# A row softmax on one core: tile-wide scaling, maxima in half tiles, and the first two loads on one queue

## The chip, the cores and the metric

The kernel runs on one core of one Trainium2 chip. The metric is the device time of one execution in microseconds (us). The median of several executions is given; executions of one kernel mostly agree within 0.3%. A profile shows one execution; its span is about 1.7 us shorter than the timed value of that execution, because the timed value holds a little around it.

Engines by their names in the profile: DVE is VectorE, ACT is ScalarE, SP is SyncE. SPq and ACTq are their sequencers, which issue the DMAs. In the DMA view q1 is the queue of SyncE and q10 that of ScalarE. A packet is one record of that view: here one partition's contiguous piece of a transfer, and beside these a few of 4 bytes at the end of each DMA. A window counts a packet where it starts. A transfer has landed when the semaphore that waits for it is complete. An issue is the instruction that starts a transfer.

## The reference

```python
x = randn(16, 1024, 512)            # float32, 33.55 MB
x_scaled = x / 2.0
exp_x = exp(x_scaled - max(x_scaled, axis=-1))
return exp_x / sum(exp_x, axis=-1)
```

A softmax over rows of 512. The 16384 rows are dealt out over 128 partitions, 128 rows to each, and each byte is read once and written once.

## The kernel before

Ten tiles, each a contiguous run of rows per partition, go through an arena in SBUF that holds 100 rows per partition: tile 0 has 3 rows per partition, tile 1 has 7, tiles 2 to 8 have 15 and tile 9 has 13. A tile is one load and one store. A tile is worked on in chunks of a few rows. VectorE takes the row maxima of a chunk, ScalarE computes the exponentials and their sums row by row, and VectorE scales by the reciprocal of the sum two chunks later.

```python
PLAN = [   # (rows of each chunk), place in the arena
    ([3], 0), ([4, 3], 3), ([5] * 3, 10), ([5] * 3, 25), ([5] * 3, 40), ([5] * 3, 55),
    ([5] * 3, 70), ([5] * 3, 85), ([5] * 3, 0), ([5, 4, 4], 15),
]
LAG = 2
SPREAD = 1            # tile 1: its last row is loaded apart
AFTER = {8: 4, 9: 6}  # load of tile 8 issued after tile 4's exponentials, 9 after 6's
FUSED = {1, 2, 3}

# issue_loads
if t == 0:
    nc.sync.dma_start(out=sb(t), in_=dram(xf, t)).then_inc(ld[t], 16)
elif t == SPREAD:
    r = tiles[t][1] - 1
    for p, q, lo, hi in ((0, P, 0, r), (0, 126, r, r + 1), (126, P, r, r + 1)):
        nc.scalar.dma_start(...)
else:
    nc.scalar.dma_start(out=sb(t), in_=dram(xf, t)).then_inc(ld[t], 16)

# do_mul(k), one chunk of c rows
nc.vector.reciprocal(...)
if t in FUSED:
    nc.vector.tensor_mul(out=arena[:, a:a+c], in0=arena[:, a:a+c],
        in1=recip[:, b:b+c].unsqueeze(2).to_broadcast([P, c, D]))
    return
for r in range(c):
    nc.vector.tensor_scalar_mul(out=arena[:, a+r], in0=arena[:, a+r],
                                scalar1=recip[:, b+r : b+r+1])

# ... VectorE's order:
for k in range(len(chunks) + LAG):
    if k < len(chunks): do_max(k)
    if k >= LAG:        do_mul(k - LAG)
```

The loads of tiles 0 and 1 are issued ahead of the barrier with which the program opens, those of tiles 2 to 7 right behind it. Tile 0's load is on SyncE's sequencer, all other loads are on ScalarE's, and all stores on SyncE's. (Cuts are marked by dots.)

## Time and profile before

| | before |
|---|---|
| time, median of the first 3 executions | 161.64 us |
| span of the profile | 159.9 us |
| DMA: bytes, rate in mid-run | 67.1 MB, 431 GB/s |
| VectorE's first maximum of tile 1 / of tile 2 | 9.39 / 18.26 us |
| VectorE's last scaling ends | 144.74 us |
| from there to the end of the span | 15.2 us |

The profile's lines are in the prediction.

### The profile page before, as it was taken

Reading aid. Unit: us, or ns where it says so; the run is one execution under the profiler, and the core shown is the slowest. Engines: PE = TensorE matmul, PEld = TensorE weight load, DVE = VectorE, ACT = ScalarE, POOL = GpSimd, SP = SyncE. Lnnn points to the kernel's source line nnn. Section 1 sums busy time; section 2 is a strip of 40 time slices with the busy share of each in tenths; the row PEclk is TensorE's granted clock in tenths of the full one; section 3 lists DMA queues with packets and bytes.
Section 4 is the critical chain, followed back from the end, with each engine's and each line's share of the span. In section 5 each row is a group of like instructions: output and inputs, shape, how many; then the busy total and the mean of one; then the engine's idle time right before and its main releaser. Section 6 shows DMA issues by size and latency. Waiting matters only on the chain.

```text
span 159.9 us, 476 instructions
## 1 busy us (share of the span) xinstructions
DVE 131.6 (82%) x153; ACT 94.4 (59%) x257; POOL 0.2 (0%) x4
## 2 busy tenths in 40 slices
DVE  0376499999999999999999999999999799992000
ACT  0369176768448547766688666786667948650000
POOL 0000000000000000000000000000000000000000
DMA  7998999999998989899999999998999998989993
GB/s 278 466 396 377 447 424 407 446 475 376 418 484 377 484 377 484 377 484 407 448 423 446 423 438 453 402 461 387 452 448 438 396 484 377 484 384 476 431 426 133
DMA packets 3028, 67.13 MB, mean 420 GB/s; under 512 B 337, under 2 KB 337, under 8 KB 721
## 3 DMA queue, kind: packets, MB, share of 16 engines
q1 hardware_dynamic: 1584, 34.34, 50.1%
q10 hardware_dynamic: 1440, 32.77, 48.1%
q14 instruction: 4, 0.02, 0.0%
HBM read 33.55 MB, written 33.55 MB: 420 GB/s over the span
## 4 chain that ended last, share of the span: by engine, by line
DVE 58%; DMA 31%; issue 0%; DVEq 0%; ACT 0%
DMA arena<-in_x_dram 31%; DVE negmax L105 30%; DVE arena L125 13%; DVE arena L118 13%; DVE recip L114 1%; DVEq L218 0%; ACT arena L144 0%
## 5 line engine op out<-in xcount | busy, mean ns | idle before, releaser
L144 ACT ACTIVATE arena<-arena,negmax 128x512 f32<-128x512 f32 x128 | 90.7, 710 | 42.5 <-DVE negmax L105 42.5
L105 DVE TENSOR_REDUCE negmax<-arena 128x5 f32<-128x2560 f32 (+2 forms) x27 | 72.1, 2675 | 12.2 <-DMA arena<-in_x_dram 12.2
L125 DVE TENSOR_SCALAR arena<-arena,recip 128x512 f32<-128x512 f32 x91 | 37.8, 482 | 0.7
L144 ACT ACTIVATION_READ_ACCUMULATOR arena<-arena,negmax 128x1 f32 x128 | 23.9, 187 | 0.0
L118 DVE TENSOR_TENSOR arena<-arena,recip 128x2560 f32<-128x2560 f32 (+2 forms) x8 | 21.0, 2625 | 0.3
L114 DVE RECIPROCAL recip<-sums 128x5 f32<-128x5 f32 (+2 forms) x27 | 4.8, 176 | 0.0
L144 ACT ACT_TABLE_LOAD x1 | 1.3, 1283 | 5.0 <-issue 5.0
L207 POOL MEMSET const-bfloat16-1.0<- 128x1 bf16 x1 | 0.1, 103 | 0.0
L207 POOL MEMSET const-uint8-127<- 128x1 uint8 x1 | 0.1, 103 | 0.0
L207 POOL MEMSET const-float32-1.0<- 128x1 f32 x1 | 0.1, 100 | 0.0
L207 POOL MEMSET const-float32-0.0<- 128x1 f32 x1 | 0.1, 99 | 0.2 <-issue 0.2
## 6 DMA issues: line engine op xcount, KB each, us to landing
arena<-in_x_dram ACTq DMA_DIRECT2D x7, 3840.0 KB, 42.9
out_dram<-arena SPq DMA_DIRECT2D x7, 3840.0 KB, 24.0
arena<-in_x_dram ACTq DMA_DIRECT2D x1, 3328.0 KB, 32.7
out_dram<-arena SPq DMA_DIRECT2D x1, 3328.0 KB, 14.2
out_dram<-arena SPq DMA_DIRECT2D x1, 1792.0 KB, 17.0
arena<-in_x_dram ACTq DMA_DIRECT2D x1, 1536.0 KB
arena<-in_x_dram SPq DMA_DIRECT2D x1, 768.0 KB, 6.7
out_dram<-arena SPq DMA_DIRECT2D x1, 768.0 KB, 15.5
```

Of the source, the lines that this page charges most:

```text
L105: nc.vector.reduce_max(out=negmax[:, b : b + c], in_=arena[:, a : a + c], axis=mybir.AxisListType.X, negate=True,)._wait_ge(ld[t], 48 if t ...
L114: nc.vector.reciprocal(out=recip[:, b : b + c], in_=sums[:, b : b + c])._wait_ge(s_exp, k + 1).then_inc(s_rec, 1)
L118: nc.vector.tensor_mul(out=arena[:, a : a + c], in0=arena[:, a : a + c], in1=recip[:, b : b + c].unsqueeze(2).to_broadcast([P, c, D]),)._w ...
L125: ins = nc.vector.tensor_scalar_mul(out=arena[:, a + r], in0=arena[:, a + r], scalar1=recip[:, b + r : b + r + 1],)
L144: ins = nc.scalar.activation(out=arena[:, a + r], in_=arena[:, a + r], func=mybir.ActivationFunctionType.Exp, bias=negmax[:, b + r : b + r ...
L207: nc = _bacc.Bacc("TRN2", target_bir_lowering=False, num_devices=1)
```

## The change

Its intent is to give VectorE fewer, longer instructions: one TENSOR_TENSOR scales a whole tile (tile 9 in two parts), and the maxima are taken over 8 and 7 rows in place of 5, 5 and 5. Beside it, the load of tile 1 moves from ScalarE's queue to SyncE's, behind tile 0, so that ScalarE's queue opens with tile 2.

```diff
 PLAN = [
-    ([3], 0), ([4, 3], 3), ([5] * 3, 10), ...
+    ([3], [3], 0), ([4, 3], [7], 3), ([8, 7], [15], 10), ...     # chunks, groups to scale, place
+    ([8, 7], [15], 0), ([5, 4, 4], [9, 4], 15),
 ]
+FIRST = 2
 ...
-            if t == 0:
-                nc.sync.dma_start(...)
-            elif t == SPREAD:
+            queue = nc.sync if t < FIRST else nc.scalar
+            if t == SPREAD:
 ...
-                    nc.scalar.dma_start(
+                queue.dma_start(
 ...
-    def do_mul(k):
+    def do_mul(j):
+        t, b, c, a, k = groups[j]
         nc.vector.reciprocal(...)
-        if t in FUSED:
-            nc.vector.tensor_mul(...)
-            return
-        for r in range(c):
-            ins = nc.vector.tensor_scalar_mul(...)
+        nc.vector.tensor_mul(...)          # the whole group
 ...
-            if k >= LAG:
-                do_mul(k - LAG)
+            while j < len(groups) and groups[j][4] + LAG <= k + 1:
+                do_mul(j)
+                j += 1
```

(A few constants stand twice in the changed file, without effect.)

## The prediction

> **What bounds the kernel now.** I read the page first. The span is 159.9 us and the timed median 161.64 us, so I add 1.7 us to any span that I work out below.
>
> ```profile
> DVE 131.6 (82%) x153; ACT 94.4 (59%) x257; POOL 0.2 (0%) x4
> ...
> DVE  0376499999999999999999999999999799992000
> ...
> DMA  7998999999998989899999999998999998989993
> ...
> HBM read 33.55 MB, written 33.55 MB: 420 GB/s over the span
> ```
>
> The reader sees two rows of nines. The DMA engines are busy from slice 2 to slice 39, moving 67.1 MB, which at the 431 GB/s of the middle of the run is 156 us: that is the bound. VectorE is nearly full as well, from slice 5 (about 18 us) to slice 36 (about 145 us), and idle in the first four slices and the last four. The stretch from 18 to 145 us alone:
>
> ```profile
> 18.00:145.00 127.00, 124.51 (x146) 85.88 (x236) 0.00 (x0) 1.00 1.00 431
> ```
>
> 124.5 us of 127 for VectorE (first number after the length), a DMA share of 1.00, 431 GB/s. So the two are balanced; ScalarE at 85.9 us has room. Whoever slows VectorE by a few us, or makes it start later, turns it into the sole bound. When its full stretch begins is told by the timeline of the start (start, length, what, and the idle time before it):
>
> ```profile
> 6.71 1.75 DVE L105 TENSOR_REDUCE negmax<-arena 128x3 f32<-128x1536 f32 x1 [6.71 <-DMA arena<-in_x_dram]
> ...
> 9.39 3.94 DVE L105 TENSOR_REDUCE negmax<-arena 128x4 f32<-128x2048 f32 x2 [0.93 <-DMA arena<-in_x_dram]
> ...
> 14.76 13.69 SPq L166 DMA_DIRECT2D out_dram<-arena  x2
> ...
> 18.26 2.82 DVE L105 TENSOR_REDUCE negmax<-arena 128x5 f32<-128x2560 f32 x1 [3.53 <-DMA arena<-in_x_dram]
> ```
>
> Tile 0 has landed by 6.7 us, tile 1 by 9.4 and tile 2 by 18.3; from there VectorE waits for data only once more (1.06 us, for tile 9 at 127.3 us). Last come the costs by form:
>
> ```profile
> L105 DVE TENSOR_REDUCE negmax<-arena 128x5 f32<-128x2560 f32 x22 | 61.9, 2813 | 4.6 <-DMA arena<-in_x_dram 4.6
> L125 DVE TENSOR_SCALAR arena<-arena,recip 128x512 f32<-128x512 f32 x91 | 37.8, 482 | 0.7
> ...
> L118 DVE TENSOR_TENSOR arena<-arena,recip 128x2560 f32<-128x2560 f32 x6 | 16.9, 2825 | 0.2
> ...
> L118 DVE TENSOR_TENSOR arena<-arena,recip 128x2048 f32<-128x2048 f32 x1 | 2.3, 2292 | 0.0
> L118 DVE TENSOR_TENSOR arena<-arena,recip 128x1536 f32<-128x1536 f32 x1 | 1.8, 1757 | 0.0
> ```
>
> **What the Trainium skill says.** "VectorE: DVE Perf Modes", section "The perf-mode tier table", puts fp32 tensor_scalar from SBUF at twice the rate of tensor_tensor and tensor_reduce, which stay at 1x. The trace agrees: the tensor_tensor rows grow by 1068 ns per 1024 elements (2825, 2292, 1757 ns), 1.04 ns an element, while five row-wise TENSOR_SCALARs take 2.07 us in the chain of waits, 0.81 ns an element with their overhead. The same page, section on the TRN2 errata, says that each instruction pays a fixed cost, so that fewer and longer ones save something: here 2825 - 2667 = 0.16 us for a tensor_tensor, and 2.73 - 2.67 = 0.06 us in the pitch of a maximum. "DMA: Bandwidth & Descriptors", section "Queues, rings and completion order", says that each DMA engine takes turns between the queues that have work, packet by packet. The trace agrees strikingly. Between 19 and 27 us the queue of SyncE (q1) held store 0, in pieces of 6 KB per partition, and that of ScalarE (q10) loads of 30 KB per partition:
>
> ```profile
> q10 hardware_dynamic: 92, 2.83, 81.8%
> q1 hardware_dynamic: 96, 0.59, 17.6%
> ```
>
> 92 packets against 96, but 2.83 MB against 0.59: turns are equal in packets, so small pieces get small bandwidth. That is why store 0, 768 KB, needed 15.5 us from issue to landing. Section "Why a DMA increments its semaphore by 16 and not by 1" of the same page says that such a DMA uses the largest number of engines up to 16 that divides its partitions: 14 for the 126-partition piece of tile 1, thus nine 2 KB packets on each. No view shows the engine of a packet; eight or nine makes little difference.
>
> **The change part by part.**
> (a) Scaling. Rows of tiles 0 and 4 to 9 that were scaled by TENSOR_SCALAR at 2.07 us per five go to one TENSOR_TENSOR per tile: 7680 x 1.042 ns + 0.16 = 8.16 us for 15 rows, against 3 x 2.07 = 6.21. So +1.95 us per tile, less two reciprocals (2 x 0.12) saved. For tiles 2 and 3, fused before, it is 8.16 against 3 x 2.83 = 8.49.
> (b) Maxima. 8 rows: 4096 x 1.042 + 0.06 = 4.33 us; 7 rows: 3.80. Sum 8.13 against 3 x 2.73 = 8.19: nothing.
> (c) One 15-row tile is then 8.13 + 0.12 + 8.16 = 16.4 us of VectorE, against 3 x (2.73 + 0.13 + 2.07) = 14.8 before (17.1 in tiles 2 and 3). DMA needs 2 x 3.93 MB / 431 = 18.2 us per tile, so in mid-stream (c) is hidden; it counts in the total of VectorE's chain.
> (d) That chain from the first maximum of tile 2 to the last scaling, in the new order of instructions: maxima of tiles 2 to 8, 7 x 8.13 = 56.9; scaling of tile 1, 0.12 + 3.89 = 4.0; of tiles 2 to 8, 7 x 8.28 = 58.0; tile 9: maxima 2.73 + 2.19 + 2.19 = 7.1, scaling in 9 and 4 rows with two reciprocals 4.96 + 2.29 + 0.22 = 7.5. Sum 133.5 us. Before it took 144.7 - 18.3 = 126.4 with its wait. ScalarE's exponentials (0.705 us a row, 10.6 per tile) keep up with 16.4.
> (e) The end. The last store needs about 1.1 us to its first byte, 3.41 MB / 431 = 7.9 us, and 2.7 us from the last data (157.2 us in the DMA view) to the end of the span: 11.7. Before it was 15.2, because 3.5 us of older stores lay ahead; in the new kernel store 8 is issued 9.7 us ahead of store 9 and takes 9.1, so hardly any backlog.
> (f) The loads. Before, tile 1 was on ScalarE's queue ahead of tile 2, so it met only tile 0. Now both are on SyncE's, and ScalarE's queue opens with tile 2's 30 KB packets as soon as the barrier lets it, at about 2.1 us (before: 1.97). Its first packets come some 1 to 2 us later, at 3.2 to 4.2. By then tile 0 is done or nearly (0.79 MB), and of tile 1's eight 12 KB packets per engine six to eight are left. Each takes a turn with a 30 KB packet: 42 KB at 25.3 GB/s per engine (405 GB/s, the mean of the load-only slices from 8 to 20 us) is 1.66 us, so some 11.5 us: 15.5. Then come the nine 2 KB packets of its last row, each behind a 30 KB packet of tile 3: 9 x 1.29 = 11.6: 27. With 1.3 us to land (as tile 0 before: data until 5.4, landed 6.7) tile 1 lands at about 28, against 9.4; I round down to 26 to 28, as the first packets may gain some ground. Tile 2 has landed by 18, but in VectorE's order its maxima come behind tile 1's.
> (g) VectorE then does tile 1's maxima (3.85) and tile 0's scaling (1.88) and comes to tile 2 at 27 + 5.75 = 32.7 us instead of 18.3.
> Sum: 32.7 + 133.5 + 11.7 = 178 us of span at the most literal, 180 timed. After tile 1 no load is late: tile 8 is needed at 32.7 + 94 = 127 us, and issued when tile 4's exponentials end, at about 74; tile 9 is needed at 143 and issued near 106.
>
> **The rivals.**
> A: shares equal in bytes, or tile 1 ahead of tile 2 throughout. Then tile 1 lands by 9 to 12 us, VectorE comes to tile 2 at about 18, and only (d) and (e) count: 18.3 + 133.5 + 11.7 = 163.5 of span, 165.2 timed, +2%. Against it stand the packet counts and store 0's 15.5 us; for it, that the piece of one row was split off by someone who tuned it, and 11 us would have been noticed.
> B: turns hold for the 12 KB packets but the 2 KB ones pass quickly, several in one turn (the skill page speaks of packets of several descriptors). Tile 1 lands at 17, VectorE comes to tile 2 at 22.7: 168 of span, 169.6 timed. In the trace the 2 KB packets ran only when the other queue was empty (150 small packets between 7 and 8 us), so nothing speaks for or against.
> C: DMA stays the bound and all is hidden: 161 to 162. That would need VectorE's 7 us more and its later start to fit in the 3.5 us of backlog at the end: possible only if tile 2 were scaled earlier than before.
> A gain needs a shorter transfer, and no byte is saved.
>
> **Range and chances.** I give the full mechanism about 65%, B 15%, A 13%, C 5%. The prediction is 177.5 us, a little under the literal 180 for the rounding in (f); the range 166 to 182 takes in B and A's upper edge. Faster by 2%: 0.01; within 2% (up to 164.9): 0.08; slower: 0.91.
>
> **What would show it.** Tile 1's load lands 22 to 28 us after its issue; VectorE waits 15 us or more for it between its first and second maximum, and ScalarE too; in that stretch the packet counts of the two queues are equal. From there VectorE has no wait for data, a TENSOR_TENSOR of 7680 takes 8.16 us, and the chain to the end is VectorE's but for the last store. DMA shows holes after about 70 us. I am wrong if tile 1 lands before 18 us, if VectorE waits again for loads 8 or 9, or if its 7680-element form is not 1.04 ns an element.

## More of the kernel before

After VectorE is done, only the last store is left, but older stores are still queued ahead of it. As long as that is so, VectorE may finish later without moving the end.

## The result, and the profile after

The changed kernel takes 176.84 us (median of 4 executions, 176.73 to 178.0) against 161.66 us for the kernel before in the same rounds. The ratio is 1.0956, 95% interval 1.091 to 1.1001; it is the mean time of one kernel's fast runs over that of the other's fast runs of the same rounds, so not quite the ratio of the medians. The change costs 15.2 us.

The changed kernel's page, the lines that answer to those of before:

```profile
span 175.1 us, 365 instructions
DVE 141.2 (81%) x42; ACT 92.8 (53%) x257; POOL 0.2 (0%) x4
...
DVE  0400029999999999999999999999999999999600
...
DMA  7999899999999999999999999999397059559795
```

VectorE's row was full from the sixth slice of 40; now it is nearly empty through the sixth, but for one short piece (tile 0's maxima), and then full to the thirty-seventh. DMA has holes in the last quarter. The bound has moved from DMA to VectorE, which starts late. The timeline of its start tells why:

```profile
4.45 1.75 DVE L125 TENSOR_REDUCE negmax<-arena 128x3 f32<-128x1536 f32 x1 [4.45 <-DMA arena<-in_x_dram]
24.95 3.95 DVE L125 TENSOR_REDUCE negmax<-arena 128x4 f32<-128x2048 f32 x2 [18.75 <-DMA arena<-in_x_dram]
...
30.69 8.21 DVE L125 TENSOR_REDUCE negmax<-arena 128x8 f32<-128x4096 f32 x2
```

Tile 0's data come 2.3 us earlier than before, tile 1's 15.6 us later. VectorE stands idle for 18.75 us in front of tile 1's maxima and begins tile 2 at 30.69 us in place of 18.26. Tile 2 had long landed by then: there is no wait in brackets before it. What the DMA queues did meanwhile, in the stretch from 14 to 16 us (queue, packets, MB):

```profile
q10 hardware_dynamic: 32, 0.98, 121.1%
q1 hardware_dynamic: 26, 0.05, 7.1%
```

32 packets of 30 KB for ScalarE's queue, 26 of 2 KB for SyncE's: nearly the same count, and a twentieth of the bytes. The forms on VectorE:

```profile
L137 DVE TENSOR_TENSOR arena<-arena,recip 128x7680 f32<-128x7680 f32 x7 | 57.1, 8158 | 0.2
L125 DVE TENSOR_REDUCE negmax<-arena 128x8 f32<-128x4096 f32 x7 | 30.9, 4412 | 0.0
L125 DVE TENSOR_REDUCE negmax<-arena 128x7 f32<-128x3584 f32 x7 | 27.1, 3876 | 0.0
L125 DVE TENSOR_REDUCE negmax<-arena 128x4 f32<-128x2048 f32 x3 | 6.8, 2280 | 18.8 <-DMA arena<-in_x_dram 18.8
```

The scaling of 15 rows takes 8.158 us. The last column is the idle time before the group: only the maxima of tile 1 (and of tile 0, 4.5 us) waited for data. And the end, from the timeline:

```profile
162.47 2.29 DVE L137 TENSOR_TENSOR arena<-arena,recip 128x2048 f32<-128x2048 f32 x1
```

VectorE ends at 162.47 + 2.29 = 164.76 us, and the span 10.3 us later, where it was 15.2 before.

### The profile page after: what moved, and what is told of

Read it like the earlier page. It is cut to its first block, busy times and chain, and to the rows that moved or that the text cites. A ratio compares the mean times of both kernels' runs of the same rounds, so it can differ in the third digit from the quotient of the medians.

```text
span 175.1 us, 365 instructions
## 1 busy us (share of the span) xinstructions
DVE 141.2 (81%) x42; ACT 92.8 (53%) x257; POOL 0.2 (0%) x4
## 4 chain that ended last, share of the span: by engine, by line
DVE 80%; DMA 13%; SPq 1%; issue 0%
DVE arena L137 40%; DVE negmax L125 39%; DMA arena<-in_x_dram 13%; DVE recip L134 1%; SPq L119 1%
## 5 line engine op out<-in xcount | busy, mean ns | idle before, releaser
L125 DVE TENSOR_REDUCE negmax<-arena 128x8 f32<-128x4096 f32 (+4 forms) x20 | 70.4, 3558 | 23.2 <-DMA arena<-in_x_dram 23.2
L137 DVE TENSOR_TENSOR arena<-arena,recip 128x7680 f32<-128x7680 f32 (+4 forms) x11 | 70.0, 6364 | 0.4
L134 DVE RECIPROCAL recip<-sums 128x15 f32<-128x15 f32 (+4 forms) x11 | 2.4, 220 | 0.0
```

The costliest lines, as they stand in the source:

```text
L125: nc.vector.reduce_max(out=negmax[:, b : b + c], in_=arena[:, a : a + c], axis=mybir.AxisListType.X, negate=True,)._wait_ge(ld[t], 48 if t ...
L134: nc.vector.reciprocal(out=recip[:, b : b + c], in_=sums[:, b : b + c])._wait_ge(s_exp, k).then_inc(s_rec, 1)
L137: nc.vector.tensor_mul(out=arena[:, a : a + c], in0=arena[:, a : a + c], in1=recip[:, b : b + c].unsqueeze(2).to_broadcast([P, c, D]),)._w ...
```

## The experiments

Two theories stood at the outset. The first is the prediction's: the two queues take turns packet by packet, so that tile 1's small packets crawl behind tile 2's and 3's large ones, VectorE starts late, and its own longer chain adds the rest. The rival says that VectorE's slower scaling form and its coarser pieces carry most of the loss, while a late load is hidden by a kernel that was bound by DMA anyway. (The edits are cut to their core; the semaphore counts that go with them are left out.)

### The changed kernel with tile 1 back on ScalarE's queue

```diff
-            queue = nc.sync if t < FIRST else nc.scalar
+            queue = nc.sync if t == 0 else nc.scalar
```

> The changed kernel with one thing undone: tile 1's load is on ScalarE's queue ahead of tile 2 again. Theory (packets of the two queues take turns, so tile 1's small packets wait behind tile 2's and 3's 30 KB ones): tile 1 lands near 9.4 us, VectorE comes to tile 2 at 18 to 19 us, its chain of 134 us and an end of 10 to 12 us follow: 164 to 165.5 us, a loss of about 2% left. Rival (VectorE's slower scaling and coarser pieces carry most of the loss): 172 us or more.

Measured: 164.41 us, ratio to before 1.0167 (1.0152 to 1.0182). Two lines of its timeline, VectorE at tile 1 and at tile 2:

```profile
9.19 3.95 DVE L125 TENSOR_REDUCE negmax<-arena 128x4 f32<-128x2048 f32 x2 [1.18 <-DMA arena<-in_x_dram]
...
18.14 8.21 DVE L125 TENSOR_REDUCE negmax<-arena 128x8 f32<-128x4096 f32 x2 [3.13 <-DMA arena<-in_x_dram]
```

The start is that of before. With VectorE's part of the change whole, 12.4 of the 15.2 us are gone, and 2.7 are left. The rival falls. (The 2.7 us are clear of noise.)

### The kernel before with only the load moved

```diff
-                    nc.scalar.dma_start(          # the three pieces of tile 1
+                    nc.sync.dma_start(
```

> The kernel before with the loads' part alone: tile 1 moved to SyncE's queue. Theory: tile 1 lands near 25 us, VectorE comes to tile 2 near 30 instead of 18.3, its chain of 125 us follows, and 3.5 us of the delay vanish in the backlog of stores: 167 to 169.5 us. Rival (the delay of the start is hidden by the balanced middle): 161 to 163 us.

Measured: 168.84 us, ratio 1.0436 (1.0419 to 1.0453). Its VectorE timeline at tile 1:

```profile
26.26 3.95 DVE L105 TENSOR_REDUCE negmax<-arena 128x4 f32<-128x2048 f32 x2 [20.05 <-DMA arena<-in_x_dram]
```

VectorE comes to tile 2 at 31.52 us, 13.3 us late, and the time grows by 7.2. Of the other 6.1 us, 1.2 are saved in VectorE's chain (125.3 us from tile 2's start in place of 126.5: it no longer waits for tile 9), and 4.9 are the slack at the end, worked out below. (The profiled execution took 170.06 us, somewhat above the other four at 168.6 to 169.0.)

### Tile 1 in one piece, still on SyncE's queue

```diff
-            if t == SPREAD:
+            if t == -1:          # tile 1 as 128 packets of 14 KB, no row split off
```

> The changed kernel, tile 1 still on SyncE's queue but loaded in one piece of 14 KB per partition, without the split-off row of 2 KB packets. Theory: the nine turns of 2 KB packets are gone, tile 1 lands at 12 to 14 us, and the time is 164 to 166 us. Rival (sharing by bytes, or any load on SyncE's queue is late): tile 1 lands at 20 us or later, 172 us or more.

Measured: 168.69 us, ratio 1.0432 (1.0416 to 1.0447). VectorE at tile 1:

```profile
16.85 3.95 DVE L125 TENSOR_REDUCE negmax<-arena 128x4 f32<-128x2048 f32 x2 [10.60 <-DMA arena<-in_x_dram]
```

This lies between the two expectations: 8.1 us come back from joining the row to the rest, which the rival did not foresee, but the landing is 3 us later than I expected. With two issues fewer ahead of the barrier (SyncE's last one ends at 0.85 us in place of 1.70), ScalarE's first load is issued at 1.25 us in place of 2.20. From 4 to 6 us the DMA view already counts 16 packets of it, against 3 in the changed kernel:

```profile
q10 hardware_dynamic: 16, 0.49, 57.4%
q1 hardware_dynamic: 35, 0.47, 57.2%
```

More of tile 1's packets therefore had to take turns than I had allowed.

### The row of small packets first

```diff
-                parts = (0, P, 0, r), (0, 126, r, r + 1), (126, P, r, r + 1)
+                parts = (0, 126, r, r + 1), (126, P, r, r + 1), (0, P, 0, r)
```

> The changed kernel with the three pieces of tile 1 issued in another order: the row of 2 KB packets first, the 12 KB packets after it. Same bytes, same packets, same queue. Theory: the small packets pass while the queue is alone (before 5.7 us), only some 12 KB packets take turns, tile 1 lands at 12 to 14 us: 164 to 166 us. Rival (bytes or the queue decide): no change, 176 to 178 us.

Measured, one look: 170.72 us; tile 1's maxima start at 18.82 us. The order alone is worth 6.1 us of time, so neither bytes nor queue decide by themselves. But it is a miss in size. Between 3 and 5 us the 2 KB packets kept the queue busy at 0.34 and 0.27 MB per us, where the changed kernel moved 0.46 and 0.41; by 6 us only 43 of the 128 packets of 12 KB had started (1 before 4 us, 19 from 4 to 5, 23 from 5 to 6), against 90 in the changed kernel, and most of the other 85 took turns.

### Smaller packets on the other queue

```diff
-                parts = ((0, P, 0, tiles[t][1]),)
+                step = 5 if t in (2, 3) else tiles[t][1]
+                parts = [(0, P, lo, lo + step) for lo in range(0, tiles[t][1], step)]
```

> The changed kernel, with the loads of tiles 2 and 3 (what tile 1 competes with) each cut into three of 5 rows, so packets of 10 KB in place of 30 KB. Theory of turns: each of the nine 2 KB packets waits for 10 KB (about 0.5 us) and not 30 KB: tile 1 lands at 14 to 16.5 us in place of 25, time 165.5 to 168.5 us. Rival (shares of bandwidth or a fixed delay): tile 1 still lands near 25, 176 to 178 us.

Measured, one look: 166.41 us. Tile 1's maxima start at 14.53 us in place of 24.95:

```profile
14.53 3.95 DVE L126 TENSOR_REDUCE negmax<-arena 128x4 f32<-128x2048 f32 x2 [8.39 <-DMA arena<-in_x_dram]
```

Nothing about tile 1's own load was touched, and the first packet of ScalarE's queue starts at 5.76 us (5.75 in the changed kernel); only the packets that tile 1 takes turns with shrank from 30 to 10 KB. This is the sharpest evidence for turns by packet.

### Twice the packets, the same bytes

```diff
-                parts = (0, P, 0, r), (0, 126, r, r + 1), (126, P, r, r + 1)
+                parts = (0, P, 0, r), (126, P, r, r + 1)
+            for half in (slice(0, 256), slice(256, 512)) if t == SPREAD else ():
+                queue.dma_start(out=sb(t)[0:126, r:r+1, half], in_=dram(xf, t)[0:126, r:r+1, half]) ...
```

> The changed kernel with tile 1's last row loaded as two halves of 1 KB per partition: the same bytes in twice the packets, eighteen turns per engine in place of nine. Theory of turns: tile 1 lands 11 to 14 us later, at 36 to 39 us, and the time is 188 to 191 us. Rival (bytes decide): unchanged, 176 to 178 us.

Measured, one look: 185.22 us. VectorE at tile 1, and from 12 to 16 us the two queues, whose counts are again near each other:

```profile
33.32 3.95 DVE L130 TENSOR_REDUCE negmax<-arena 128x4 f32<-128x2048 f32 x2 [27.08 <-DMA arena<-in_x_dram]
...
q10 hardware_dynamic: 53, 1.63, 95.4%
q1 hardware_dynamic: 44, 0.05, 3.2%
```

The direction is the theory's, and the rival (bytes decide) falls; the size is less than I expected, 8.4 us for nine more turns, or 0.93 us a turn where I had reckoned with 1.2 to 1.5. ScalarE's first load was issued 0.57 us later here (2.77 against 2.20 us), so its packets start later (6.25 against 5.75 us) and tile 1's pass alone for longer, which may be part of it. The rest I cannot settle: no view shows packets by engine.

### The kernel before with only the scaling changed

```diff
-    ([3], [3], 0), ([4, 3], [7], 3), ([8, 7], [15], 10), ...
+    ([3], [3], 0), ([4, 3], [7], 3), ([5] * 3, [15], 10), ...   # and tile 1 on ScalarE's queue
```

> The kernel before with the scaling's part alone: one TENSOR_TENSOR per tile, maxima in fives as before, tile 1 on ScalarE's queue. Theory: the whole of what the changed kernel loses beside the load is here: VectorE's chain is 134 us from 18.3 us: 163.5 to 165.5 us. Rival (the slower form is hidden by DMA): 161.3 to 162.3 us.

Measured: 165.21 us, ratio 1.0216 (1.0199 to 1.0234). Its first maxima of tile 2, and its last scaling:

```profile
18.28 5.54 DVE L125 TENSOR_REDUCE negmax<-arena 128x5 f32<-128x2560 f32 x2 [3.09 <-DMA arena<-in_x_dram]
...
150.50 2.29 DVE L137 TENSOR_TENSOR arena<-arena,recip 128x2048 f32<-128x2048 f32 x1
```

VectorE ends at 152.79 us; the span ends 10.3 us later, at 163.1. The rival (hidden by DMA) falls. The kernel takes 0.8 us more than the version with the larger maxima (164.41 us; of this 0.6 us lie in the span): the scaling is the part that costs, and the larger maxima, given that scaling, save a little.

### Form or grain

```diff
-        nc.vector.tensor_mul(out=arena[:, a : a + c], ...)     # one per group
+        for r in range(c):
+            ins = nc.vector.tensor_scalar_mul(out=arena[:, a + r], ...)   # one per row, same groups
```

> The changed kernel with tile 1 on ScalarE's queue and the scaling by one TENSOR_SCALAR per row, a whole tile at a time: it tells the form from the grain. If the form costs (1.04 ns an element against 0.81), VectorE needs some 14.5 us per tile, DMA bounds again: 161 to 162.5 us. If the grain of a whole tile costs (stores later), 163.5 us or more, as with the tile-wide instruction.

(Tile 1 is on ScalarE's queue here too.) Measured: 161.6 us, ratio 1.0001 (0.9983 to 1.0018). Its costliest forms:

```profile
L138 DVE TENSOR_SCALAR arena<-arena,recip 128x512 f32<-128x512 f32 x128 | 51.7, 482 | 0.4
L125 DVE TENSOR_REDUCE negmax<-arena 128x8 f32<-128x4096 f32 x7 | 30.9, 4418 | 13.5 <-DMA arena<-in_x_dram 13.5
```

VectorE now waits 13.5 us for data before its 8-row maxima: it runs ahead of DMA, which bounds again. So scaling a whole tile late costs no time here, and the slower form of the instruction does: the 128 short instructions are busy for 51.7 us, the 11 long ones of the changed kernel for 70.0.

### The kernel before with only the maxima changed

```diff
-    ([3], [3], 0), ([4, 3], [7], 3), ([8, 7], [15], 10), ...
+    ([3], [3], 0), ([4, 3], [4, 3], 3), ([8, 7], [8, 7], 10), ...   # scaled chunk by chunk, as before
```

> The kernel before with the maxima's part alone: 8 and 7 rows at a time, each followed by its own scaling in before's forms. Theory: VectorE's sum is unchanged within 1 us and DMA bounds: 161.2 to 162.3 us, same. Rival (coarser maxima delay the first stores and ScalarE): 163 us or more.

Measured: 161.83, 162.67, 168.59 and 170.33 us, the last two classed as slow. (On one core that class rests on the time alone, over 1.5% above the fastest run.) That is no clean answer: the best runs are at before's time, as expected, but before itself had nothing like the two others on the same chip. So it ran again, with a variant:

> The maxima-only kernel again, unchanged, because its four runs split into 161.8 and 162.7 and two near 169. If the two late ones were a chance of that session: all runs at 161.6 to 162.7 us. If the kernel itself is fragile: again some runs several us above the others, while the kernel before, on the same chip, stays within 0.3 us.

Measured: 169.65, 161.92, 164.09, 164.49, 166.22 and 168.47 us, while the kernel before stayed at 161.50 to 161.82. It is the kernel that is fragile. A slow execution was profiled this time. Beside a fast one it shows where its time went, not why. Two of its waits:

```profile
DVE negmax L125 <- DMA arena<-in_x_dram: 20.6, 5, 6.7
ACT arena L164 <- DMA out_dram<-arena: 7.1, 1, 7.1
```

VectorE waited 20.6 us for loads (13.9 in the fast profile), and ScalarE stood 7.1 us (4.4) in front of tile 8's load until store 2 had landed. The variant takes that stand away:

```diff
-AFTER = {8: 4, 9: 6}
+AFTER = {8: 5, 9: 6}
```

> The maxima-only kernel with the load of tile 8 issued after tile 5's exponentials and not tile 4's, so that ScalarE does not stand 4.4 us in front of it until store 2 has landed. If that stand is what makes the maxima-only kernel fragile, all runs are at 161.3 to 162.5 us; if something else does, the spread stays.

Measured: 161.7, 165.88, 168.46, 163.65, 168.21 and 162.48 us. Its profiled execution, a fast one, has no such wait, and the spread stays: that explanation fell, as far as one profile can say that the wait is gone in all of them. In the slow profile tile 9's load took 38.7 us from issue to landing, against 34.1 in the fast one, and the last VectorE chain starts from it. Why the late loads lose ground to the stores in some executions and not in others is left open. The changed kernel shows no such spread (176.73 to 178.0 us), and in its profile VectorE waits for no load after tile 1.

## Why the prediction was right

The mechanism was right: turns by packet made tile 1 late, VectorE waited for it, and its own longer chain followed to the end. That 177.5 us met 176.84 so closely is in part luck. The literal sum was 179.6 timed; its three terms were off by 2.0 us too much (tile 2's start), 0.6 too little (the chain) and 1.4 too much (the end), and the rounding down to 177.5 took off most of the difference. The sum can be checked term by term, because a single rule holds through all variants with a tile-wide TENSOR_TENSOR: the span is the time at which VectorE begins tile 2, plus 134 us, plus 10.3 us.

| kernel | tile 1's maxima start | tile 2's start | VectorE ends | span |
|---|---|---|---|---|
| before | 9.39 | 18.26 | 144.74 | 159.9 |
| changed | 24.95 | 30.69 | 164.76 | 175.1 |
| changed, tile 1 on ScalarE's queue | 9.19 | 18.14 | 152.21 | 162.5 |
| changed, 10 KB packets on the other queue | 14.53 | 20.27 | 154.34 | 164.6 |
| changed, tile 1 in one piece | 16.85 | 22.59 | 156.67 | 167.0 |
| changed, row first | 18.82 | 24.56 | 158.64 | 168.9 |
| changed, row in two halves | 33.32 | 39.06 | 173.13 | 183.4 |

All in us, read from the timelines. In the last six rows tile 2's start to VectorE's end is 134.07 or 134.08, and VectorE's end to the span's 10.3.

- (a) to (d), VectorE's chain. Predicted 133.5, measured 134.1. One 15-row scaling was predicted at 8.16 and took 8.158 us. The missing half microsecond is the reciprocals of 15 rows: 0.19 us in the chain with its issue gap, where 0.12 was carried over from 5 rows, seven times. That the chain costs time, although the middle was bound by DMA, was shown by the scaling-only kernel and, from the other side, by the row-wise one. Two readings on the way were not borne out. VectorE was not idle in the first four slices (its row begins 0376). And the skill's factor of two for tensor_scalar is shown by no run: every TENSOR_SCALAR here has 512 elements, at 0.81 ns an element with its overhead.
- (e), the end. Predicted 11.7, measured 10.3: this term was mis-sized by 1.4 us. The part that was off is the tail of 2.7 us. It was read from the DMA view as if 157.2 us were the end of the data, but the view counts a packet where it starts. By the records of the trace, which have each packet's length, the last data of before end at 158.55 us, 1.35 before the end of the span, and those of the changed kernel at 173.71, again 1.35 before it. There the last store has 0.8 us to its first packet and 8.1 us of data. That the backlog of before would be gone was right, and it explains how the parts add. Before had 15.2 - 10.3 = 4.9 us of slack after VectorE. The late start costs 12.4 us of VectorE's time and the longer chain 134.1 - 126.5 = 7.6; less 4.9 that is 15.1, and 15.2 was measured. The scaling-only kernel confirms the slack: VectorE ends 8.05 us later than in before, the span 3.2. Alone, each part hides behind that slack: the load costs 7.2 us by itself and the scaling 3.5, together 10.7 and not 15.2.
- (f), the landing of tile 1. Predicted 26 to 28 us, measured 24.95; the mechanism was shown by the 10 KB packets, the halved row and the one piece. But two terms within it were wrong and partly cancelled. ScalarE's first packets were to come at 3.2 to 4.2 us; the first is at 5.75 us, 3.5 us after its issue, so by 6 us 90 of the 128 packets of 12 KB had started, nearly all alone, and not a quarter of them at most. The profile of before held the warning. Its store 0, issued at 14.76 us beside ScalarE's loads, has its first packet at 18.45 us (none of its queue from 17.5 to 18 us, 4 from 18 to 18.5), so in 3.7 of its 15.5 us none of its packets had started. In the profiles of ten kernels (all but the three with only the maxima changed) store 0's first packet comes 3.4 to 4.1 us after its issue. Why is open. The nine turns of the row were to take 11.6 us; its packets started from 9.6 to 23.2 us, 13.6 us in all. (A slip beside these: 42 KB at 25.3 GB/s is 1.70 us, not 1.66, with the KB of 1024 bytes that the next term uses.) Two of the expectations that I missed, for the one piece and for the row first, failed at the first term: how much passes before the other queue wakes. The third, for the halved row, was too high by about 3 us. The 14 engines for the piece of 126 partitions fit the trace: if each DMA leaves one packet of 4 bytes per engine, the counts come out: 336 over all DMAs in the changed kernel, 320 with tile 1 in one piece, 350 with one more piece of 126.
- (g) Predicted 5.75 us from tile 1's landing to tile 2's start: 5.74 in the changed kernel.
- Rival A (equal shares, 165.2 us) and C (all hidden) are refuted by the counts and by the time. Rival B, in which small packets pass several in a turn, is refuted by the counts from 14 to 16 us and by the halved row, which should then have cost next to nothing. A's remark that somebody would have noticed 11 us was no evidence.
- Of the signs that I named, one was wrong: DMA was to show holes after about 70 us. They begin at about 122 us. This is the window from 120 us on (length, VectorE, ScalarE, POOL, clock, DMA share, GB/s):

```profile
120.00:140.00 20.00, 19.97 (x5) 14.21 (x41) 0.00 (x0) 1.00 0.59 255
```

That step was a guess, worked out nowhere; a count of bytes would have corrected it. Loads 0 to 7 and stores 0 to 2 are 32.8 MB, 76 us of work at 431 GB/s, and by then store 3 (75.9 us) and tile 8's load (79.4 us) were issued. Nothing in the sum rested on it.

No experiment beat the kernel before. It moves its bytes at 431 GB/s with hardly a hole, and the row-wise version that gives VectorE 8 us of air (123.3 us busy against 131.6) has the same time.

## What to carry to other kernels

In these runs, with two DMA queues busy, a transfer's landing time followed from how many packets it had and how large the other queue's packets were, not from its bytes alone. So try to put the load that everything waits for ahead of the large ones in the same queue (tile 1's maxima at 9.19 us in place of 24.95), to give it fewer and larger packets (16.85), or to give its rivals smaller ones (14.53). Fewer instructions are no gain for VectorE if the longer form is slower per element; count elements times ns before counting instructions. In a kernel whose two bounds are balanced, find out how much later the second one may end before the span moves, since parts of a change hide behind that slack only once.

## What the Trainium skill lacked or had wrong

- "DMA: Bandwidth & Descriptors", sections "Issuing engines are not separate DMA queues" and "Rules for kernel authors": the choice of the issuing engine is said to save only issue time. No run here gained bandwidth by it, so that stands; but it leaves out when a transfer lands. Here moving one load to the other queue changed its landing from 9.4 to 25 us, and made the kernel before 4.4% slower when done alone.
- The same page, "Queues, rings and completion order", has the turns by packet right, but does not draw the consequence, which is that shares follow packet size: 0.05 MB against 0.98 MB in 2 us at 26 against 32 packets. It speaks of packets of 9 to 17 descriptors; the records here count one packet for each partition's contiguous piece, from 1 to 30 KB.
- The same page, "Latency and other measured facts", gives about 600 ns to the first byte for this path. With the DMA engines free that fits: in the changed kernel the first packet of SyncE's first load starts at 1.03 us, 0.65 us after the issuing instruction ends (0.38 us), and the last store's 0.5 us after. No page has the delay beside a busy queue: ScalarE's first load there has its first packet 3.2 us after its issuing instruction ends (2.58 to 5.75 us).
- "VectorE: DVE Perf Modes", section on the TRN2 errata, needs no correction for tensor_tensor: from its formula, checked there at 512 and 2048 elements, (N + 151) cycles at 0.96 GHz, comes an estimate of 8157 ns for 7680 elements, and 8158 were measured.
